# The opening of a transformer layer kernel: squares summed in fours, later copies, a dot row and sums interleaved, and the context's columns loaded later

## The chip, the cores and the metric

The kernel runs on one core of a Trainium2 chip. A core has a matrix engine (TensorE, PE in the profile, its weight loads PEld), VectorE (DVE), ScalarE (ACT), GpSimd (POOL) and SyncE (SP), which here issues the loads. The engines run side by side, each through its own queue in order. The metric is the device time of one execution in microseconds (us).

## The reference

One layer of a backbone over 512 latent tokens and 256 context tokens, width 1024. All vectors are modulated: two conditioning vectors, `c` for latent tokens and `c_ctx` for context tokens, go through SiLU and a matrix `w_ada` of 1024 x 9216, which gives shifts, scales and gates. The opening of the kernel belongs to the first sublayer:

```python
mx = jnp.split((jax.nn.silu(c) @ w_ada + b_ada)[:, None, :], N_MOD, axis=-1)
mc = jnp.split((jax.nn.silu(c_ctx) @ w_ada + b_ada)[None, None, :], N_MOD, axis=-1)
...
def rms_norm(x, w):
    y = xf * lax.rsqrt(jnp.mean(xf * xf, axis=-1, keepdims=True) + EPS)
    return (y * w.astype(jnp.float32)).astype(x.dtype)
...
h = modulate(rms_norm(h_in, norm_w), shift, scale)      # h * (1 + scale) + shift
return h_in + 0.5 * gate * swiglu(h, w1, w3, w2)
```

After it come token mixing (latent attention in one head group, a gated chunk MLP in the other) and a second such sublayer; the output is the latent stream.

## The kernel before

All activations lie transposed, features on the 128 partitions and tokens along the row: `x` holds eight blocks k of 128 features with 768 columns, in two groups g of 256 latent and 128 context tokens each. A product in fp32 precision is made of three matmuls over high and low parts (`hh`, `hl` for the activation, `oph`, `opl` for the weight; `op5h` and `op5l` are the pair of k=5). The opening, up to about 67 us, has to get from nothing to the first four output blocks of the first up-projection, and works on the eight feature blocks as they come.

**Loads.** SP issues in the written order: x's latent columns in five loads; then for each block k a unit of three: scale (a block of `w_ada` for TensorE, three buffers), shift (a block of `w_ada` for VectorE, two k to a tile), raw (the weights of the first products, three buffers). `first_units(k)` issues the three. The context's columns of x come in two loads of four blocks: the first behind the units of k = 0, 1, 2, the second inside the unit of k = 3, between its scale and its shift.

**Spread vectors.** TensorE spreads both SiLU vectors over all partitions (L499, into `big`), and `put_cb(w)` on ScalarE copies them to `cb`, where the dot products with the shifts read them. The same two banks later hold the first products.

**Norm.** `square0(0, k)` makes the square of block k of the latent columns: on ScalarE, except that of k = 3, which VectorE makes, and that of k = 7, of which each engine makes a half. Squares lie in a pool of four buffers (`sqx0`), which the context's squares and the pair of k=5 use too. VectorE adds squares, and `sums` (L460) lets TensorE add over the partitions by a matmul with ones, each into the two halves of the columns (`sumx`). Before: squares 0 and 1 are added and summed, 2 and 3 are added and summed, 4, 5 and 6 are added, 7 stands alone; `late_sums(g)` sums these last two for half g. `root(g)` on ScalarE and `steps(g)` on VectorE make the reciprocal root.

**Modulation of block d.** `ada_row(d)` (L320, sixteen records on TensorE) multiplies both vectors with the scale block; `ada_copy(d)` takes the row out of PSUM on ScalarE; `ada_col` (L329) turns it into a column, and ScalarE makes of it the factor `a`. `ada_sum(d, which)` on VectorE is the dot product of the shift block with a spread vector (tile `junk`, 128x1024), and `ada_s` on ScalarE adds the bias. `which` is 0 for latent and 1 for context tokens.

**Block k's operand.** `first_x` (VectorE, `hfull`) multiplies x, the root and the factor; `first_h` (ScalarE) adds the shift and rounds to `hh`; `first_l` (VectorE) makes `hl`. `first_half(g)` (L580) are the products of k = 0 by halves; `step_mm(k)` (L588) those of the others; `first_ctx(k)` (L573) those of the context's columns.

**Steps.** `step_open(k)` stands at the head of each step on TensorE: the column of block k+1 and the dot row of block k+2; `step_mm(k)` ends it. Between them the code writes what VectorE and ScalarE do for the next blocks. The context's squares are made in this time, by `square1(j)` on ScalarE (four blocks j over the 256 columns), added by `ctx_add(a, b)` on VectorE into the third, folded once, and summed by TensorE in step 4, ahead of `step_mm(4)`.

The order on ScalarE, VectorE and TensorE is the written one throughout the opening, as is SP's. A buffer of a pool is given by a planner, which runs through the program with modelled times, and an instruction that needs a buffer waits until its last reader is done. Behind the opening most of the kernel is ordered by hand as well; between the two feed-forward sublayers some parts of the token mixing (lines 1443 to 1612) are ordered by the planner.

Of the kernel before, what the change touches and what calls it, by code (L numbers as in the profile page):

```python
# [9 lines left out]
F32 = mybir.dt.float32  # L10
# [23 lines left out]
W1 = 2 * NFIRST * P  # L34
# [139 lines left out]
def layer_kernel(ctx: ExitStack, tc: tile.TileContext, xT, wfirst, wst, wada, wuq, wkpe, cols, wrope, vnw, rope, out):  # L174
    nc = Core(tc)
# [18 lines left out]
    def big():  # L194
        return half[0].tile([P, 2, 512], F32, tag="big", bufs=2, name=f"big_{nc.next_id()}")
# [59 lines left out]
    load_x = lambda k, n, c: pin(nc.sync.dma_start(four(x[:, k : k + n, :], c), four(xT[:, k : k + n, :], c)))  # L255
    for k, n in ((0, 2), (2, 2), (4, 2), (6, 1), (7, 1)):
        load_x(k, n, slice(0, 256))
    sblk, units = [], []

    def first_units(k, between=None):  # L260
        ra = sp.tile([P, D], F32, tag="sa", bufs=3, name=f"scale_{k}")
        pin(nc.sync.dma_start(ra, wada[k][:, :D]))
        if between:
            between()
        if k % 2 == 0:
            pool, tag, bufs = (sp, "sb", 1) if k == 4 else (st.raw_pool, "block", BLOCKS)
            sblk.append(pool.tile([P, 2048], F32, tag=tag, bufs=bufs, name=f"shift_{k}"))
        rs_ = sblk[-1][:, (k % 2) * D : (k % 2) * D + D]
        pin(nc.sync.dma_start(rs_, wada[k][:, D:]))
        rw = st.raw()  # L270
        pin(nc.sync.dma_start(rw[:, :W1], wfirst[k]))
        units.append((ra, rs_, rw[:, :W1]))

    for k in range(3):
        first_units(k)
    load_x(0, 4, slice(256, 384))
    warm = mm()
    nc.scalar.activation(epsc2, epsc, AF.Silu)
    for i in range(4):
# [38 lines left out]
    def ada_row(d):  # L318
        for kt in range(NK):
            pin(nc.tensor.matmul(pa[0:2, :P], sc[:, kt, :], units[d][0][:, kt * P : kt * P + P], start=kt == 0, stop=kt == NK - 1))  # L320

    def ada_copy(d):
        row = sp.tile([2, P], F32, tag="row", name=f"row_{d}")
        nc.scalar.copy(row, pa[0:2, :P])
        return row

    def ada_col(row, d):
        o = pcol[:, 2 * d : 2 * d + 2]
        pin(nc.tensor.matmul(o, row, ident[0:2, 0:2], start=True, stop=True))  # L329
        nc.scalar.activation(  # L330
            pairs[0][1][:, d, :], o, AF.Identity, bias=b1n[:, d : d + 1], scale=col[:, COL_N1 + d : COL_N1 + d + 1])

    def ada_sum(d, which):
        ada_dot(units[d][1], d, which, accs[:, d, which : which + 1])

    def ada_s(d, which):
        nc.scalar.activation(mod_s[0][which][:, d : d + 1], accs[:, d, which : which + 1], AF.Identity, bias=col[:, d : d + 1])

    def ada_shift(d, which):
        ada_sum(d, which)  # L340
        ada_s(d, which)
# [110 lines left out]

    def square1(j):
        sq = sp.tile([P, 512], F32, tag="sqx0", bufs=4, name=f"sq0_1{j}")
        nc.scalar.activation(
            sq.rearrange("p (q c) -> p q c", c=P), x.rearrange("p k (g c) -> p (k g) c", g=2)[:, 4 * j : 4 * j + 4, 256:384], AF.Square)
        return sq

    def sums(dst, sq, first, last):
        pin(nc.tensor.matmul(dst[:, :256], ones, sq, start=first, stop=last))  # L460
# [40 lines left out]
    sumx = [mm(), mm()]  # L501
    half_of = lambda g: slice(256 * g, 256 * g + 256)
    put_cb = lambda w: nc.scalar.copy(cb[:, w, :], bb[w].rearrange("p g c -> p (g c)"))
    for k in (0, 2):
        sa = square0(0, k)
        sb = square0(0, k + 1)
        nc.vector.tensor_add(sa, sa, sb)
        for g in range(2):
            sums(sumx[g], sa[:, half_of(g)], k == 0, False)
    put_cb(0)  # L510
    sq = [square0(0, k) for k in (4, 5, 6)]
    nc.vector.tensor_add(sq[0], sq[0], sq[1])
    nc.vector.tensor_add(sq[0], sq[0], sq[2])
    nc.vector.tensor_scalar_add(b1, col[:, COL_B : COL_B + 72], 1.0)
    sq[1] = square0(0, 7)
    put_cb(1)
    nc.vector.tensor_mul(b1n, b1[:, NK : 2 * NK], col[:, COL_N1 : COL_N1 + NK])
    ops = {}

    def oph(k):  # L520
        ops[k] = st.pair() if k != OPS else [sp.tile([P, 512], F32R, tag="sqx0", bufs=4, name=f"op5{p}") for p in "hl"]
        nc.scalar.copy(ops[k][0], units[k][2])

    def opl(k):
        nc.vector.tensor_sub(ops[k][1], units[k][2], ops[k][0].bitcast(F32))

    r0, v = rstd_tiles(0)
    rs = [v]
# [1 line left out]
    def late_sums(g):  # L530
        for i in range(2):
            sums(sumx[g], sq[i][:, half_of(g)], False, i == 1)

    def root(g):
        rstd_root(sumx[g], r0[:, half_of(g)])

    def steps(g):
        rstd_steps(sumx[g], r0[:, half_of(g)], v[:, half_of(g)])

    late_sums(0)  # L540
    root(0)
    ada_row(0)
    row = ada_copy(0)
    ada_col(row, 0)
    late_sums(1)
    oph(0)
    steps(0)
    ada_shift(0, 0)
    root(1)
    first_x(0, 0, 0)  # L550
    first_h(0, 0, 0)
    opl(0)
    first_units(3, lambda: load_x(4, 4, slice(256, 384)))
    ada_row(1)
    row = ada_copy(1)
    first_l(0, 0, 0)
# [2 lines left out]
    first_x(0, 0, 1)  # L559
    opl(1)  # L560
    first_h(0, 0, 1)
    pbs = bigs(4)
    pcs = []

# [37 lines left out]
    sqs = []  # L602
# [10 lines left out]
    ada_sum(2, 0)  # L613
    first_l(1, 0)
    oph(2)
    opl(2)
    ada_s(2, 0)
    for k in (4, 5):
        first_units(k)

    step_open(1)
    first_x(2, 0)
    first_h(2, 0)
    row = ada_copy(3)
    ada_sum(0, 1)
    for j in (0, 1):
        sqs.append(square1(j))
    first_l(2, 0)
    ada_sum(3, 0)
    oph(3)  # L630
    opl(3)
    ada_s(3, 0)
    ada_s(0, 1)
    sqs.append(square1(2))
    step_mm(1)

    step_open(2)
    first_x(3, 0)
    first_h(3, 0)
    sqs.append(square1(3))  # L640
    row = ada_copy(4)
    ctx_add(2, 0)
    first_l(3, 0)
    ada_sum(4, 0)
    oph(4)
    opl(4)
    ada_s(4, 0)
    ada_sum(1, 1)
    ada_s(1, 1)
    step_mm(2)  # L650
    for k in (6, 7):
        first_units(k)

    step_open(3)
    first_x(4, 0)
    first_h(4, 0)
    row = ada_copy(5)
    ctx_add(3, 1)
    first_l(4, 0)
    ada_sum(5, 0)  # L660
    oph(5)
    opl(5)
    ada_s(5, 0)
# [8 lines left out]
    first_h(5, 0)  # L672
    row = ada_copy(6)
    first_l(5, 0)
    ada_sum(6, 0)
    rc = rstd_tiles(1)
    rstd_root(sumc, rc[0])
    rstd_steps(sumc, *rc)
    rs.append(rc[1])
    nc.scalar.activation(epsc2, epsc, AF.Silu)  # L680
    ada_s(6, 0)
    for j in (0, 1):
        first_x(j, 1)
# [530 lines left out]
    sums = [SsqAcc(npool, 384, nc.vector) for _ in range(2)]  # L1214
# [220 lines left out]
    def between():  # L1435
        if next(slots) and tiny and next(tiny[0], tiny) is tiny:
            tiny.pop(0)
# [223 lines left out]
    steps = [(h, t) for h in range(HEADS) for t in range(4)]  # L1661
# [156 lines left out]
    for i in range(3, LAST):  # L1818
        j = i - 3
# [31 lines left out]
    i = LAST  # L1851
# [360 lines left out]
```

## Time and profile before

| | |
|---|---|
| median of 3 runs | 1134.43 us (1132.75 to 1135.95) |
| the profiled execution | 1134.94 us, its span 1133.2 us |
| granted TensorE clock | 1.000 |
| TensorE busy | 1124.0 us (99%) |
| VectorE, ScalarE, GpSimd busy | 906.4, 540.5, 306.8 us |
| moved by DMA | 125.89 MB, 111 GB/s in the mean |

The profile is of one execution. Ends of matmuls in it are modelled, so TensorE's work is best read from the starts. A row of the timeline has the start and the duration in us, the engine, the line of the code (L59 stands for everything that is recorded in written order), the operation, what is written and read, the count of merged instructions, and in brackets how long the engine was idle before and what it waited for.

### The profile page before, as it was taken

What the parts mean: (1) busy time and instruction counts of PE and PEld (TensorE: products, weight loads), DVE (VectorE), ACT (ScalarE), POOL (GpSimd) and SP (SyncE); (2) the same over time, 40 slices, a digit from 0 to 9 for tenths busy, and PEclk for the clock granted to TensorE, in tenths of its full rate; (3) what the DMA queues carried; (4) which work ended last, traced back from release to release, by engine and by line L of the source; (5) the groups of instructions that cost most, each with busy time, mean ns of one, the idle gap of its engine ahead of it and who ended that gap; (6) DMA issues with size and microseconds to landing.
All of it is one profiled execution on the core that took longest, in us unless ns stands there. A gap on an engine that the chain in (4) does not pass through costs nothing.

```text
span 1133.2 us, 18761 instructions
## 1 busy us (share of the span) xinstructions
PE 1124.0 (99%) x7078; PEld 1072.6 (95%) x7078; DVE 906.4 (80%) x1666; ACT 540.5 (48%) x1120; POOL 306.8 (27%) x268
## 2 busy tenths in 40 slices
PE   9999999999999999999999999999999999999998
PEld 7799999999999999999988889999999989898997
DVE  6989999888888779867746889978886868686884
ACT  6555422431344214445745559975544535353451
POOL 0002402321333023300018327740013435152330
PEclk9999999999999999999999999999999999999999
DMA  9630353244333755322243111002131422233312
GB/s 343 212 116 19 118 181 132 102 143 146 116 127 138 246 192 187 112 69 66 84 149 109 40 38 39 20 27 86 56 107 46 147 75 91 98 111 112 113 38 93
DMA packets 35674, 125.89 MB, mean 111 GB/s; under 512 B 3712, under 2 KB 10624, under 8 KB 30976
## 3 DMA queue, kind: packets, MB, share of 16 engines
q1 hardware_dynamic: 35440, 124.63, 32.2%
q8 instruction: 56, 0.92, 0.3%
q14 instruction: 34, 0.28, 0.1%
q10 hardware_dynamic: 144, 0.06, 0.0%
HBM read 122.58 MB, written 2.10 MB: 110 GB/s over the span
## 4 chain that ended last, share of the span: by engine, by line
PE 89%; DVE 6%; POOL 2%; issue 1%; ACT 1%; DVEq 0%; ACTq 0%; POOLq 0%
PE mm L59 54%; PE one L59 19%; PE big L59 7%; PE big L588 2%; PE mm L320 1%; DVE opl L59 1%; PE mm L573 1%; PE mm L170 1%; PE mm L169 1%; PE mm L168 1%; DVE hfB L59 1%; DVE m8k L59 1%; PE big L499 0%; POOL ut L1501 0%; PE mm L280 0%
## 5 line engine op out<-in xcount | busy, mean ns | idle before, releaser
L59 DVE TENSOR_TENSOR opl<-block,oph 128x512 fp32r<-128x512 f32 x216 | 192.3, 898 | 35.4 <-ACT oph L59 31.8
L59 POOL TENSOR_TENSOR block<-block 128x512 f32<-128x512 f32 x69 | 105.2, 1525 | 391.8 <-DVE opl L59 389.1
L59 ACT CAST oph<-block 128x512 fp32r<-128x512 f32 x216 | 133.8, 622 | 117.3 <-PE mm L59 85.4
L59 PE MATMUL mm<-gh,oph 128*128 128x384 f32 (+1 forms) x440 | 155.2, 353 | 0.0
L59 PE MATMUL mm<-gl,oph 128*128 128x384 f32 (+1 forms) x440 | 154.9, 352 | 0.0
L59 PE MATMUL mm<-gh,opl 128*128 128x384 f32 (+1 forms) x440 | 154.9, 352 | 0.0
L59 DVE SCALAR_TENSOR_TENSOR x<-mm,g,x 128x256 f32<-128x256 f32 (+2 forms) x185 | 85.4, 499 | 49.0 <-PE mm L59 48.9
L59 ACT CAST oph<-raw 128x512 fp32r<-128x512 f32 x115 | 69.9, 620 | 78.1 <-PE mm L59 56.3
L59 PEld LDWEIGHTS mm<-gh,opl 128*128 128x128 f32 x440 | 82.6, 188 | 5.7
L59 PEld LDWEIGHTS mm<-gh,oph 128*128 128x128 f32 x440 | 82.6, 188 | 5.6
L59 PEld LDWEIGHTS mm<-gl,oph 128*128 128x128 f32 x440 | 82.6, 188 | 5.5
L59 POOL TENSOR_TENSOR block<-s,block 128x512 f32<-128x512 f32 x35 | 47.8, 1367 | 142.3 <-DVE opl L59 141.4
L59 DVE TENSOR_TENSOR opl<-raw,oph 128x512 fp32r<-128x512 f32 x115 | 77.7, 691 | 8.8 <-ACT oph L59 8.0
L59 PE MATMUL mm<-hh,oph 128*128 128x384 f32 x192 | 64.5, 336 | 0.0
L59 PE MATMUL mm<-hl,oph 128*128 128x384 f32 x192 | 64.2, 334 | 0.0
L59 PE MATMUL mm<-hh,opl 128*128 128x384 f32 x192 | 64.1, 334 | 0.0
L59 DVE SCALAR_TENSOR_TENSOR junk<-raw,cb 128x1024 bf16<-128x1024 f32 x48 | 62.1, 1308 | 0.0
L59 POOL TENSOR_TENSOR s<-block 128x512 f32<-128x512 f32 x34 | 50.2, 1477 | 21.0 <-DMA block<-wst 21.0
L59 PE MATMUL one<-hh,oph 128*128 128x384 f32 x144 | 48.1, 334 | 0.0
L59 PE MATMUL one<-hl,oph 128*128 128x384 f32 x144 | 48.1, 334 | 0.0
L59 PE MATMUL one<-hh,opl 128*128 128x384 f32 x144 | 48.1, 334 | 0.0
L59 DVE SCALAR_TENSOR_TENSOR raw<-raw,cb 128x1024 f32<-128x1024 f32 x32 | 41.0, 1288 | 7.7 <-DMA raw<-wada 7.4
(683 smaller groups left out, 3430.5 us busy)
## 6 DMA issues: line engine op xcount, KB each, us to landing
raw<-wst SPq DMA_DIRECT2D x77, 512.0 KB, 3.7
block<-wst SPq DMA_DIRECT2D x36, 1024.0 KB, 4.9
raw<-wada SPq DMA_DIRECT2D x56, 512.0 KB, 4.1
scale<-wada SPq DMA_DIRECT2D x8, 512.0 KB, 8.7
shift<-wada SPq DMA_DIRECT2D x8, 512.0 KB, 9.2
x<-xT SPq DMA_DIRECT2D x5, 512.0 KB, 6.1
raw<-wfirst SPq DMA_DIRECT2D x8, 256.0 KB, 8.3
out<-x SPq DMA_DIRECT2D x7, 256.0 KB, 2.2
```

What stands on the lines that cost most here:

```text
L59: return lambda *a, **k: self.tc.keep_in_program_order(f(*a, **k))
L168: nc.tensor.matmul(out, lh, rh, start=first, stop=False, skip_group_check=more)
L169: nc.tensor.matmul(out, lh, rl, start=False, stop=False, skip_group_check=more)
L170: nc.tensor.matmul(out, ll, rh, start=False, stop=last, skip_group_check=more)
L320: pin(nc.tensor.matmul(pa[0:2, :P], sc[:, kt, :], units[d][0][:, kt * P : kt * P + P], start=kt == 0, stop=kt == NK - 1))
L573: pin(nc.tensor.matmul(o, l[:, c], r, start=k == 0 and m == 0 and w == 0, stop=k == NK - 1 and m == 2, skip_group_check=True))
L588: pin(nc.tensor.matmul(two(pbs[i]), l[:, c], lat(r, k), start=False, stop=k == NK - 1 and m == 2, skip_group_check=True))
```

## The change

The opening's order is written anew; nothing is computed by other means.

- Squares 0 to 3 are made first and added up (three adds on VectorE), and one sum per half stands for the two of before. Then squares 4 to 7 are made, all ahead of the adds of 4, 5 and 6.
- `put_cb(0)` moves behind the squares, `put_cb(1)` behind the first root.
- The rounded weights of k = 0 (`oph(0)`), the first dot product with the shift and the root's steps come ahead of the first dot row; the sums of the second half come between that row and its column.
- The units of loads are split into functions. The unit of k = 4 comes earlier, the context's columns go behind unit 4 and behind scale 5; the shifts of k = 6 and 7 go last.
- The context's squares move from steps 1 and 2 to the end of step 2 and to step 3, the adds of them into step 3, the second vector's dot product of block 1 to an earlier place in step 2, and in step 4 the dot product of block 6 behind the context's root.

```diff
+    def first_scale(k):
         ra = sp.tile([P, D], F32, tag="sa", bufs=3, name=f"scale_{k}")
         pin(nc.sync.dma_start(ra, wada[k][:, :D]))
-        if between:
-            between()
+        units.append([ra])
+
+    def first_shift(k):
...
+    def first_units(k):
+        first_scale(k)
+        first_shift(k)
+        first_raw(k)
     for k in range(3):
         first_units(k)
-    load_x(0, 4, slice(256, 384))
...
-    for k in (0, 2):
-        sa = square0(0, k)
-        sb = square0(0, k + 1)
-        nc.vector.tensor_add(sa, sa, sb)
-        for g in range(2):
-            sums(sumx[g], sa[:, half_of(g)], k == 0, False)
-    put_cb(0)
-    sq = [square0(0, k) for k in (4, 5, 6)]
+    sq = [square0(0, k) for k in range(4)]
+    for i, j in ((1, 0), (3, 2), (3, 1)):
+        nc.vector.tensor_add(sq[i], sq[i], sq[j])
+    for g in range(2):
+        sums(sumx[g], sq[3][:, half_of(g)], True, False)
+    sq = [square0(0, k) for k in (4, 5, 6, 7)]
     nc.vector.tensor_add(sq[0], sq[0], sq[1])
     nc.vector.tensor_add(sq[0], sq[0], sq[2])
+    sq[1] = sq[3]
+    put_cb(0)
     nc.vector.tensor_scalar_add(b1, col[:, COL_B : COL_B + 72], 1.0)
-    sq[1] = square0(0, 7)
-    put_cb(1)
...
     late_sums(0)
     root(0)
+    put_cb(1)
+    oph(0)
+    ada_sum(0, 0)
+    steps(0)
     ada_row(0)
     row = ada_copy(0)
+    ada_s(0, 0)
+    late_sums(1)
     ada_col(row, 0)
-    late_sums(1)
-    oph(0)
-    steps(0)
-    ada_shift(0, 0)
     root(1)
     first_x(0, 0, 0)
     first_h(0, 0, 0)
     opl(0)
-    first_units(3, lambda: load_x(4, 4, slice(256, 384)))
+    first_units(3)
...
     first_h(0, 0, 1)
+    first_units(4)
+    load_x(0, 4, slice(256, 384))
...
     ada_s(2, 0)
-    for k in (4, 5):
-        first_units(k)
+    first_scale(5)
+    load_x(4, 4, slice(256, 384))
+    first_shift(5)
+    first_raw(5)
     step_open(1)
...
     ada_sum(0, 1)
-    for j in (0, 1):
-        sqs.append(square1(j))
...
     ada_s(0, 1)
-    sqs.append(square1(2))
     step_mm(1)
     step_open(2)
     first_x(3, 0)
     first_h(3, 0)
-    sqs.append(square1(3))
     row = ada_copy(4)
-    ctx_add(2, 0)
+    ada_sum(1, 1)
     first_l(3, 0)
     ada_sum(4, 0)
     oph(4)
     opl(4)
     ada_s(4, 0)
-    ada_sum(1, 1)
     ada_s(1, 1)
+    for j in (0, 1):
+        sqs.append(square1(j))
     step_mm(2)
     for k in (6, 7):
-        first_units(k)
+        first_scale(k)
+        first_raw(k)
+    for k in (6, 7):
+        first_shift(k)
     step_open(3)
     first_x(4, 0)
     first_h(4, 0)
     row = ada_copy(5)
-    ctx_add(3, 1)
+    for j in (2, 3):
+        sqs.append(square1(j))
+    ctx_add(2, 0)
     first_l(4, 0)
     ada_sum(5, 0)
+    ctx_add(3, 1)
     oph(5)
     opl(5)
     ada_s(5, 0)
...
     first_l(5, 0)
-    ada_sum(6, 0)
     rc = rstd_tiles(1)
     rstd_root(sumc, rc[0])
     rstd_steps(sumc, *rc)
     rs.append(rc[1])
     nc.scalar.activation(epsc2, epsc, AF.Silu)
+    ada_sum(6, 0)
     ada_s(6, 0)
```

More of the change, by code (lines that the diff above doesn't have):

```diff
@@ L257, in layer_kernel @@
         load_x(k, n, slice(0, 256))
-    sblk, units = [], []
-    def first_units(k, between=None):
+    sblk, units, raws_ = [], [], []
+    def first_scale(k):
         ra = sp.tile([P, D], F32, tag="sa", bufs=3, name=f"scale_{k}")
         pin(nc.sync.dma_start(ra, wada[k][:, :D]))
-        if between:
-            between()
+        units.append([ra])
+    def first_shift(k):
         if k % 2 == 0:
@@ L269, in first_units, with first_raw @@
         pin(nc.sync.dma_start(rs_, wada[k][:, D:]))
+        units[k].append(rs_)
+    def first_raw(k):
         rw = st.raw()
         pin(nc.sync.dma_start(rw[:, :W1], wfirst[k]))
-        units.append((ra, rs_, rw[:, :W1]))
+        raws_.append(rw[:, :W1])
+    def first_units(k):
+        first_scale(k)
+        first_shift(k)
+        first_raw(k)
     for k in range(3):
         first_units(k)
-    load_x(0, 4, slice(256, 384))
     warm = mm()
@@ L521, in oph @@
         ops[k] = st.pair() if k != OPS else [sp.tile([P, 512], F32R, tag="sqx0", bufs=4, name=f"op5{p}") for p in "hl"]
-        nc.scalar.copy(ops[k][0], units[k][2])
+        nc.scalar.copy(ops[k][0], raws_[k])
     def opl(k):
-        nc.vector.tensor_sub(ops[k][1], units[k][2], ops[k][0].bitcast(F32))
+        nc.vector.tensor_sub(ops[k][1], raws_[k], ops[k][0].bitcast(F32))
     r0, v = rstd_tiles(0)
```

## Prediction, made before the changed kernel ran

> **What bounds the kernel now.** I read the page first, then the busy time by stretches, then the opening's timeline engine by engine.
>
> ```profile
> PE 1124.0 (99%) x7078; PEld 1072.6 (95%) x7078; DVE 906.4 (80%) x1666; ACT 540.5 (48%) x1120; POOL 306.8 (27%) x268
> ...
> PE 89%; DVE 6%; POOL 2%; issue 1%; ACT 1%; DVEq 0%; ACTq 0%; POOLq 0%
> ```
>
> The first line is the busy time of each engine, the second the chain that ended last. TensorE is the bound nearly everywhere, so an edit of the opening counts only by what it does to TensorE: matmuls taken out, waits taken out, waits put in. Next, one stretch of the busy times (length, then busy PE, PEld, DVE, ACT, POOL).
>
> ```profile
> 49.00:67.00 18.00, 18.00 (x124) 16.62 (x124) 17.38 (x33) 8.95 (x22) 0.00 (x0) 1.00 0.54 177
> ```
>
> TensorE has no gap in these last 18 us of the opening, but VectorE is busy 17.38 of them: it keeps pace and can't give back a delay there. What can be won lies before, in the timeline of the opening (start, duration, engine, line, operation, count, idle before and its releaser).
>
> ```profile
> 1.03 3.78 PE L280 MATMUL mm<-ones 128*128 128x256 f32 x8 [1.03 <-DVE nhalf L224]
> ...
> 6.26 0.69 DVE L59 TENSOR_TENSOR sq<-sq,sq 128x512 f32<-128x512 f32 x1 [5.26 <-ACT sq L59]
> ...
> 6.39 0.63 ACT L59 ACTIVATE sq<-x 128x512 f32<-128x512 f32 x1 [0.17 <-DMA x<-xT]
> 6.87 0.68 DVE L59 TENSOR_TENSOR sq<-x 128x512 f32<-128x512 f32 x1
> ...
> 7.67 1.01 ACT L59 COPY cb<-big 128x1024 f32<-128x1024 f32 x1 [0.65 <-PE big L499]
> ...
> 9.26 1.89 PE L460 MATMUL mm<-sq,ones 128*128 128x256 f32 x8
> ...
> 10.32 0.94 ACT L59 ACTIVATE sq<-x 128x512 f32<-128x512 f32 x2 [0.59 <-PE mm L460]
> ...
> 11.70 0.42 DVE L59 TENSOR_TENSOR sq<-x 128x256 f32<-128x256 f32 x1
> ...
> 11.73 1.14 PE L460 MATMUL mm<-sq,ones 128*128 128x256 f32 x4 [0.58 <-DVE sq L59]
> ...
> 12.80 1.91 PE L320 MATMUL mm<-scale,sc 128*2 128x128 f32 x16
> ...
> 15.05 0.38 PE L329 MATMUL mm<-ident,row 2*128 2x2 f32 x2 [0.34 <-ACT row L59]
> ...
> 15.47 0.35 ACT L59 ACTIVATE a<-mm,b1n,col 128x2 f32<-128x2 f32 x1 [0.47 <-PE mm L329]
> ...
> 16.42 1.91 PE L320 MATMUL mm<-scale,sc 128*2 128x128 f32 x16
> ...
> 16.90 0.50 ACT L59 ACTIVATE hh<-hfull,s 128x256 fp32r<-128x256 f32 x1
> ...
> 17.43 0.49 DVE L59 SCALAR_TENSOR_TENSOR hl<-hfull,s,hh 128x256 fp32r<-128x256 f32 x1 [0.38 <-ACT hh L59]
> ...
> 18.26 0.74 PE L580 MATMUL big<-hh,oph 128*128 128x256 f32 x4
> ```
>
> Between 9.26 and 18.26 TensorE waits 0.58 us for a sum of squares and 0.34 us for the copied row; the eight records at 9.26 are the sums of two pairs. All that the opening holds is therefore 0.58 + 0.34 + half of 1.89 (0.95), some 1.9 us.
>
> **The first sums.** Four squares are added first, so four records stand for eight: 0.95 us of TensorE work goes. VectorE's square of k=3 needs the load that ScalarE's third square waits for (6.39), so it runs from 6.39 to 7.07 (0.68); the adds of 0.69 us follow some 0.6 us apart (6.26 to 6.87 is that step), and the third reads the second's result: start 8.4, end 9.1. TensorE is at the spread vectors until 9.26, so it waits for nothing here.
>
> **The second sums.** The pool of squares has four buffers. At 10.32 ScalarE's square waits for TensorE's first four records of sums, which release a buffer. In the new order the same four records read the buffer of square 3, the last of the four that comes free, and the eighth square takes it: again at 10.32. VectorE does half of that square (0.42), and both adds of the second group now stand behind it in its queue: 10.33, then about 10.7 and 11.4 (the second add reads the first's result), end 12.1. TensorE starts the late sums at about 12.15, 0.4 us later than 11.73. If the planner gives the eighth square the buffer of square 1 instead (free at 9.1, when square 6 asks too), it is 11.73 as before; so 0 to +0.45, and I take +0.4, since buffers come free in this order and square 6 asks first. The freed 0.95 us thus turns into a longer wait: TensorE idles from about 10.3 to 12.15.
>
> **Row and sums interleaved.** From 11.73 to 16.42 TensorE needed 4.69 us, with the 0.34 us and some 0.06 us around the row copy idle. Second sums now fill that hole: 12.15 + 4.69 - 0.4 = 16.4, no gain against 16.42. The scale's column moves behind those sums, from 15.05 to 16.0, so `a` starts at 16.4 instead of 15.47; then x's product (0.49, as the row at 17.43), hh (0.50) until 17.85, hl (0.49) until 18.4. TensorE wants hh at 18.2 and hl one group (0.58) later: 0.4 us of cover in both, and what goes beyond it costs one to one. Copies of the spread vectors behind the squares: the first (1.01) starts behind the eighth square's half, near 10.7, and ends near 11.7, before its reader, the dot product with the shift, which VectorE reaches after 12.1; the second runs while VectorE makes the first root's steps. Cost nothing, for the same cover. Opening in sum: 0, from -0.4 to +0.5.
>
> **SP's queue.** Of each unit three transfers; context's x (two of 512 KB) goes behind unit 4's and behind scale 5.
>
> ```profile
> 14.74 0.61 SPq L262 DMA_DIRECT2D scale<-wada  x1
> ...
> 23.95 1.91 PE L320 MATMUL mm<-scale,sc 128*2 128x128 f32 x16
> ...
> scale<-wada SPq DMA_DIRECT2D x8, 512.0 KB, 8.7
> ...
> x<-xT SPq DMA_DIRECT2D x5, 512.0 KB, 6.1
> ```
>
> Scale 3 goes out at 14.74 and with the median 8.7 us lands near 23.4, used at 23.95: cover about 0.5. With one x transfer fewer ahead of it this can only widen. The x transfers wait on SP behind scales that need a freed buffer, the last of them that of the third dot row, which is over before the fourth starts at 23.95; so they leave by about 24 and land by about 30 (6.1), and the squares of them move to 34 and later. No queue comes late: 0. The shifts of 6 and 7 no longer hold raw 6 and scale 7 back: 0 too, since TensorE has no wait there.
>
> **Context's squares and their adds.** Here a cost lies on the path. Step 3 before:
>
> ```profile
> 26.45 1.15 ACT L59 ACTIVATE sq<-x 128x512 f32<-128x512 f32 x2
> ...
> 32.11 1.22 DVE L59 SCALAR_TENSOR_TENSOR junk<-shift,cb 128x1024 bf16<-128x1024 f32 x1
> ...
> 33.85 0.38 PE L329 MATMUL mm<-ident,row 2*128 2x2 f32 x2
> ...
> 35.32 0.34 ACT L59 ACTIVATE a<-mm,b1n,col 128x2 f32<-128x2 f32 x1
> ...
> 36.48 0.72 ACT L59 ACTIVATE hh<-hfull,s 128x512 fp32r<-128x512 f32 x1 [0.82 <-DVE hfull L59]
> ...
> 37.10 0.24 ACT L59 COPY row<-mm 2x128 f32<-2x128 f32 x1
> ...
> 37.23 0.75 DVE L59 SCALAR_TENSOR_TENSOR hl<-hfull,s,hh 128x512 fp32r<-128x512 f32 x1 [0.19 <-ACT hh L59]
> ...
> 37.90 1.22 DVE L59 SCALAR_TENSOR_TENSOR junk<-shift,cb 128x1024 bf16<-128x1024 f32 x1
> ...
> 39.05 0.69 DVE L59 TENSOR_TENSOR op5l<-raw,op5h 128x512 fp32r<-128x512 f32 x1
> 39.65 0.68 DVE L59 TENSOR_TENSOR sq<-sq,sq 128x512 f32<-128x512 f32 x1
> 40.37 0.42 DVE L59 TENSOR_TENSOR sq<-sq 128x256 f32<-128x256 f32 x1
> 40.71 0.74 DVE L59 SCALAR_TENSOR_TENSOR hfull<-x,a,v 128x512 f32<-128x512 f32 x1
> ...
> 41.11 0.70 PE L460 MATMUL mm<-sq,ones 128*128 128x256 f32 x2
> ```
>
> The folded square ends at 40.37 + 0.42 = 40.8, and TensorE reads it at 41.11 ahead of step 4's matmuls: 0.3 us of cover. After: step 2's last dot product ends near 33.5 (32.11 + 1.22, and 0.2 for the other one pulled ahead of it), ScalarE then makes two bias columns and squares 0 and 1 (1.15) until about 35.2, `a` until 35.45, x's product (0.74, as at 40.71) 35.5 to 36.25, hh 36.3 to 37.0, the row, and only then squares 2 and 3 (1.15): 37.1 to 38.25. VectorE's first add (2 with 0) waits for square 2 until 37.75, with nothing to do since 36.25, and the queue stands behind it: add 37.75, hl 38.35, dot product 39.0, add 40.15, low operand 40.75, add 41.35, fold 42.05 to 42.5 (steps by starts: 0.6 for an add or operand, 0.67 for hl, 1.15 for a dot product). TensorE's sums go from 41.11 to 42.5: **+1.4 us**. Bounds: +1.0 if ScalarE passes the squares 0.4 us sooner, +1.8 if the operand copy for k=5, which needs a square's buffer, adds what it can.
>
> **After that.** VectorE is 42.45 - 40.71, so 1.7 us late, and stays late through a stretch without gaps; where hl of context's k=2 goes to TensorE, there was a wait before:
>
> ```profile
> 53.11 0.19 PEld L573 LDWEIGHTS mm<-hl,oph 128*128 128x128 f32 x1 [0.15 <-DVE hl L59]
> ```
>
> VectorE recovers part (its root steps now go ahead of a dot product, one stall on ScalarE's root less), so I put +0.1 there, between 0 and +0.3. The kernel behind 67 us moves as a block. Sum: 0 + 1.4 + 0.1 = +1.5 us. The profiled execution took 1134.94 us, so 1136.4; the median of the runs shown, 1134.43, is 0.5 below it: **1135.9**. By the bounds: +0.6 to +2.6, so 1135.0 to 1137.0. A measurement tells 0.3% (3.4 us) from no change, so this is no change.
>
> **A gap and the clock.** Two rows bear on whether 1.9 us of idle TensorE slow it down:
>
> ```profile
> 663.19 0.47 PE L59 MATMUL mm<-mixh,oph 128*128 128x512 f32 x1 [1.60 <-ACT uo0h L59]
> 663.50 0.39 PE L59 MATMUL mm<-mixl,oph 128*128 128x512 f32 x1
> 640.00:680.00 40.00, 37.85 (x200) 31.96 (x199) 35.19 (x71) 22.30 (x45) 9.19 (x12) 1.00 0.12 40
> ```
>
> After 1.60 us of idleness the next matmul follows 0.31 us later and the granted clock of the stretch is 1.00. The Trainium skill, page "TensorE: Matmul & The Clock Gate", section "Part 1: The HAM clock gate", has the array fall to half clock after at least one idle window of about 3.4 us; by that rule a gap of 1.9 us costs nothing, and the sum stays; the trace agrees as far as 1.60 us.
>
> **Rivals.**
> *The clock drops in the new gap* (slower). Eight records of 128x256 took 3.78 us at the start and 1.89 us from 9.26, so cold is half pace. It stayed cold for those 3.78 us at least; as long a cold stretch from 12.15 loses half of that, 1.9 us, and up to half of 8.2, 4.1 us, if it lasts as long as from 1.03 to 9.26. With +1.5: 1137.8 to 1140.0, say 1138.5. It decides from a gap longer than the 1.60 us seen to be free, and the new one is. Chance 0.12.
> *The adds come in time* (the change's plain reading): square 2 earlier, or the second sums not behind the eighth square. Then the waits of 0.58 and 0.34 us and the 0.95 us are won in part: 1132.5 to 1134.8. For it speaks that VectorE's and ScalarE's waits in steps 2 and 3 are short; against it the written order, which those engines follow. Chance 0.16.
> *The planner answers.* The order of lines 1443 to 1612 (token mixing, ahead of the stretch from 640 us) isn't written by hand but planned from modelled times, so a changed opening can turn it. TensorE idles 2.15 us in that stretch: winning it with the 1.9 us of the opening gives 1130.4, losing as much again on top of +1.5 gives 1138.1. Nothing in the profile says which. Chance 0.32: 0.11 faster, 0.09 within 0.3%, 0.12 slower.
>
> **How the numbers follow.** The forecast keeps 0.40. Within 0.3%: 0.40 + 0.16 + 0.09 = 0.65; slower: 0.12 + 0.12 = 0.24; faster 0.11. The range runs from 1132.0 (most of the early case) to 1139.0 (most of the clock and planner cases).
>
> **What would show it.** Right: four sum records from 9.26; TensorE's next at 12.1 with a wait on VectorE; the second dot row at 16.4; a wait of over 1 us on VectorE before the two sums of step 4; from there all matmuls about 1.5 us later. Wrong: the late sums at 11.7 or earlier; no wait at step 4; 128x128 dot rows that take near 3.8 instead of 1.91 us (clock); or equal openings and another time in the token mixing (planner).

## The result, and the profile after

The changed kernel takes 1138.27 us (median of 7 executions, 1136.92 to 1141.34) against 1134.35 us before (7 executions, 1132.55 to 1135.95): the ratio is 1.0041, with a 95% interval of 1.0032 to 1.0051. It is slower by about 3.9 us, which a measurement can tell from no change; the forecast was 1135.9 us and "no change". The profiled execution of the changed kernel is its longest, 1141.34 us with a span of 1139.6.

From the page of the changed kernel, the busy time of the engines and the chain that ended last; then, from the busy times by stretches, the one that answers to 49 to 67 us (length, busy PE, PEld, DVE, ACT, POOL, granted clock, DMA share, GB/s):

```profile
PE 1126.7 (99%) x7074; PEld 1073.3 (94%) x7074; DVE 907.6 (80%) x1667; ACT 540.7 (47%) x1120; POOL 306.9 (27%) x268
...
PE 85%; DVE 7%; ACT 2%; issue 1%; DMA 1%; POOL 0%; ACTq 0%; DVEq 0%; POOLq 0%
...
53.00:71.00 18.00, 17.99 (x121) 16.42 (x120) 17.41 (x34) 8.99 (x22) 0.00 (x0) 1.00 0.51 172
```

TensorE is busy for 2.7 us more than before although the change takes matmuls out: a first sign that the same matmuls ran more slowly. The stretch behind the opening looks as it did. The opening itself is told by TensorE's timeline (start, duration, engine, line, operation, count, idle before and its releaser). All lines of the opening lie eight to ten further down than before: L468 are the sums, L328 the dot rows, L337 the column, L590 the first products.

```profile
9.31 1.13 PE L468 MATMUL mm<-sq,ones 128*128 128x256 f32 x4 [0.71 <-DVE sq L59]
12.36 2.08 PE L468 MATMUL mm<-sq,ones 128*128 128x256 f32 x4 [1.92 <-DVE sq L59]
14.37 3.57 PE L328 MATMUL mm<-scale,sc 128*2 128x128 f32 x16
17.87 1.44 PE L468 MATMUL mm<-sq,ones 128*128 128x256 f32 x4
19.24 0.38 PE L337 MATMUL mm<-ident,row 2*128 2x2 f32 x2
19.55 1.91 PE L328 MATMUL mm<-scale,sc 128*2 128x128 f32 x16
```

The four records of the first sums start where they should, and the late sums at 12.36 (forecast 12.15) behind a gap of 1.92 us. Then come rows that are too long, although TensorE waits for nothing inside them: 2.08 instead of 1.14 us for four sums, 3.57 instead of 1.91 us for the first dot row. The second dot row starts 3.13 us later than before (16.42). At 19.55 us the same form takes 1.91 us again. This is a lower clock, not a wait, and the stretches show it. Their edges are laid on the edges of the half-clock stretches, which are 3.41 us or twice that long:

```profile
8.30:11.71 3.41, 1.43 (x7) 0.79 (x5) 2.05 (x5) 2.83 (x5) 0.00 (x0) 1.00 1.05 400
11.71:15.12 3.41, 2.76 (x8) 1.64 (x9) 2.16 (x6) 0.73 (x3) 0.00 (x0) 0.50 1.04 406
15.12:18.53 3.41, 3.41 (x16) 1.97 (x14) 1.13 (x3) 1.70 (x4) 0.00 (x0) 0.50 0.95 372
18.53:21.94 3.41, 3.41 (x26) 2.47 (x25) 1.88 (x4) 1.67 (x5) 0.00 (x0) 1.00 0.80 272
667.07:670.48 3.41, 1.71 (x7) 1.33 (x8) 3.41 (x8) 1.94 (x4) 0.05 (x1) 1.00 0.30 98
670.48:673.89 3.41, 3.41 (x10) 2.74 (x10) 1.14 (x3) 0.00 (x0) 0.00 (x0) 0.50 0.17 60
```

The granted clock is 0.50 from 11.71 to 18.53 us, and once more from 670.48 to 673.89, behind the gap of 1.60 us of which the prediction had said that it costs nothing. The stretch ahead of each fall is one in which TensorE was busy for half of the time or less: 1.43 and 1.71 of 3.41 us. Before, the same gap of 1.60 us lay across an edge:

```profile
658.80:662.21 3.41, 2.42 (x15) 1.73 (x14) 3.38 (x8) 1.59 (x5) 1.23 (x2) 1.00 0.02 5
662.21:665.62 3.41, 2.43 (x11) 2.02 (x12) 3.02 (x6) 0.99 (x3) 0.00 (x0) 1.00 0.42 156
```

These are stretches of the kernel before, with the edges counted on by 3.413 us from the start of its full clock at 6.86 us. Each half of the gap leaves 2.4 us of work in its stretch, and the clock stays full.

The rest of the loss is in step 3. From the timelines of VectorE, ScalarE and TensorE:

```profile
38.57 0.75 DVE L59 SCALAR_TENSOR_TENSOR hfull<-x,a,v 128x512 f32<-128x512 f32 x1 [1.23 <-ACT a L59]
...
40.13 1.15 ACT L59 ACTIVATE sq<-x 128x512 f32<-128x512 f32 x2
...
40.79 0.69 DVE L59 TENSOR_TENSOR sq<-sq,sq 128x512 f32<-128x512 f32 x1 [1.47 <-ACT sq L59]
...
45.31 0.43 DVE L59 TENSOR_TENSOR sq<-sq 128x256 f32<-128x256 f32 x1
...
45.88 0.67 PE L468 MATMUL mm<-sq,ones 128*128 128x256 f32 x2 [1.58 <-DVE sq L59]
```

VectorE stands 1.47 us behind ScalarE's square 2, its fold ends at 45.7, and TensorE waits 1.58 us for it ahead of the two sums of step 4, where it waited for nothing before.

Followed along TensorE in this execution, the delay against before is 3.1 us at the second dot row, 4.8 us at the sums of step 4, 5.9 us at 637 us and 7.5 us at 674 us; between 878 and 906 us some 1.0 us comes back, where the kernel before has short waits of its own that the later arrival absorbs; 6.4 us are left. This is the longest execution; the medians lie 3.9 us apart. The 1.1 us at 637 us are a wait of 1.52 instead of 0.44 us, whose chain goes back to two loads of weights (3.79 and 4.50 us from issue to landing). Behind 80 us the order of the instructions on TensorE, VectorE, ScalarE and GpSimd is that of before.

### The profile page after: what moved, and what is told of

Read it like the earlier page. It is cut to its first block, busy times and chain, and to the rows that moved or that the text cites. A ratio compares the mean times of both kernels' runs of the same rounds, so it can differ in the third digit from the quotient of the medians.

```text
span 1139.6 us, 18757 instructions
## 1 busy us (share of the span) xinstructions
PE 1126.7 (99%) x7074; PEld 1073.3 (94%) x7074; DVE 907.6 (80%) x1667; ACT 540.7 (47%) x1120; POOL 306.9 (27%) x268
## 4 chain that ended last, share of the span: by engine, by line
PE 85%; DVE 7%; ACT 2%; issue 1%; DMA 1%; POOL 0%; ACTq 0%; DVEq 0%; POOLq 0%
PE mm L59 54%; PE one L59 19%; PE big L59 7%; PE mm L583 1%; DVE opl L59 1%; PE big L598 1%; PE mm L170 1%; PE mm L168 1%; PE mm L169 1%; DMA raw<-wst 1%; DVE hfB L59 1%; DVE m8k L59 1%; DVE opl L140 0%; DVE ut L1522 0%; DVE hfA L59 0%
```

## The experiments

Two theories at first. **C**: the gap of 1.92 us makes TensorE's clock fall, and this is the larger part of the loss. **S**: the late fold of context's squares makes the rest. Rivals were **V**, that VectorE's and ScalarE's chain in the opening is late by itself; **X**, that the context part makes the loss and the opening is made up for later; and **Q**, that the new order of the loads costs something. All medians below are of 6 or 11 executions, and each group of kernels ran beside the kernel before on the same chip (1134.04, 1133.44 and 1134.29 us in the three groups). Each execution also lists its mean granted clock; half clock for one stretch of 3.41 us shows as 0.998.

### Work in the gap

```diff
     for g in range(2):
         sums(sumx[g], sq[3][:, half_of(g)], True, False)
+    for _ in range(4):          # 2 in the second kernel
+        pin(nc.tensor.matmul(two(pa[:, :256]), ones, ones2, start=True, stop=True))
```

Four matmuls of ones, expected:

> The changed kernel with four matmuls of ones (128x256, results never read) behind the first sums, 4 x 0.47 = 1.9 us, so that TensorE has work from 10.4 to 12.3 us. Theory C (the idle 1.92 us of TensorE made its granted clock fall to half for 6.83 us): the clock stays full through the opening, the late sums start within 0.2 us of 12.36, the first dot row takes 1.91 instead of 3.57 us and the second starts near 16.5 instead of 19.55; the wait of 1.6 us ahead of the sums of step 4 stays; 1135.2 to 1136.2 us. Rival V (VectorE's and ScalarE's chain in the opening is late by itself, and the clock only goes along with it): the second dot row stays at 19 or later and the time at 1138.

Two of them, expected:

> As the kernel with four matmuls of ones, but with two (0.95 us), so that about 1.0 us of idleness is left ahead of the late sums. Theory C with a threshold (it takes more than about 1.3 us idle of a stretch of 3.4 us): the clock stays full, second dot row near 16.5, 1135.2 to 1136.2 us. If any gap of about 1 us behind the first sums is enough: half clock again for 3.4 or 6.8 us, second dot row 18 to 19.5, 1137 to 1138.3 us. Rival V: 1138.

Measured: 1136.36 us with four (ratio to before 1.0017, interval 1.0009 to 1.0026) and 1135.63 us with two (1.0014, 1.0005 to 1.0023). TensorE's timeline with four, then the late sums and the second dot row with two:

```profile
10.23 1.89 PE L518 MATMUL mm<-ones 128*128 128x256 f32 x8
12.31 1.13 PE L468 MATMUL mm<-sq,ones 128*128 128x256 f32 x4 [0.19 <-DVE sq L59]
13.38 1.91 PE L328 MATMUL mm<-scale,sc 128*2 128x128 f32 x16
...
16.58 1.91 PE L328 MATMUL mm<-scale,sc 128*2 128x128 f32 x16
...
42.93 0.67 PE L468 MATMUL mm<-sq,ones 128*128 128x256 f32 x2 [1.58 <-DVE sq L59]
```

```profile
12.20 1.13 PE L468 MATMUL mm<-sq,ones 128*128 128x256 f32 x4 [1.05 <-DVE sq L59]
...
16.46 1.91 PE L328 MATMUL mm<-scale,sc 128*2 128x128 f32 x16
```

The late sums start when they did, VectorE is no faster, and yet the second dot row comes 3.0 us earlier. V falls: with the same chain on VectorE and ScalarE the opening costs 0.2 us at most (second dot row at 16.58 and 16.46, against 16.42 before). Half of the gap (1.05 us) does no harm, so it is not the gap as such. The time is the expected one in the second kernel and 0.2 us above the band in the first. Each against its own runs of before, the filled gap wins 1.6 and 2.3 us of the 3.9. The wait of 1.58 us in step 4 stays, as expected. So does the kernel's own gap of 1.60 us: both profiles fall to half clock once, behind it, at 665.70 and 665.57 us.

### Each half of the change alone

The opening of the change in the kernel before (squares, sums, copies, dot row; loads and context as before), and the context part alone (loads, squares, adds, with the opening of before):

> The kernel before with the opening of the change alone (four squares added ahead of their sums, copies of the spread vectors behind the squares, row and sums interleaved); loads, squares and adds of context stay as before. Theory C: gap of 1.9 us, half clock for 3.4 to 6.8 us, second dot row at 18.5 to 19.6, no wait over 0.5 us ahead of the sums of step 4 unless VectorE is late; all behind 20 us later by about 3; 1137.0 to 1137.8 us. Rival X (the context part makes the loss, the opening is made up for later): within 0.7 us of the kernel before, 1133.7 to 1135.1 us.

> The kernel before with the context part of the change alone: context's x loaded later, its squares and adds in steps 2 and 3 at the places of the change; the opening as before. Theory S (the fold of context's squares comes too late): clock full throughout, a wait of 1.0 to 1.8 us on VectorE ahead of the two sums of step 4, all behind it later by that; 1135.4 to 1136.2 us. Rival C alone (only the clock counts, the wait of step 4 is made up behind it): within 0.5 us of the kernel before. Rival Q (the order of the loads holds something up behind 60 us): over 1136.5 us, with a DMA as releaser.

Measured: 1136.12 us for the opening alone (1.0019, 1.0011 to 1.0028) and 1135.94 us for the context part alone (1.0015, 1.0005 to 1.0024). The opening alone, TensorE's timeline and two stretches:

```profile
12.29 1.22 PE L460 MATMUL mm<-sq,ones 128*128 128x256 f32 x4 [1.92 <-DVE sq L59]
13.45 3.44 PE L320 MATMUL mm<-scale,sc 128*2 128x128 f32 x16
...
18.18 1.91 PE L320 MATMUL mm<-scale,sc 128*2 128x128 f32 x16
```

```profile
9.78:13.19 3.41, 1.50 (x7) 0.87 (x5) 2.64 (x6) 1.39 (x3) 0.00 (x0) 1.00 1.03 404
13.19:16.60 3.41, 3.41 (x17) 1.86 (x16) 1.79 (x5) 1.90 (x3) 0.00 (x0) 0.50 1.03 404
...
661.73:665.14 3.41, 1.76 (x12) 1.18 (x11) 3.41 (x8) 1.62 (x4) 1.23 (x2) 1.00 0.01 2
```

The same gap of 1.92 us, but one stretch at half clock instead of two, and the second dot row at 18.18: the cost of the same gap differs from execution to execution. The gap at 664 us lay with 1.76 us of work in its stretch and did not lower the clock. The median is 0.9 us below the expected 1137.0, because not every execution falls, or falls twice: 2 of 11 had a mean clock of 1.000 (mean 1134.49 us), 5 had 0.998 (1135.70), 3 had 0.997 (1137.41) and one 0.995 (1138.81). The time follows the clock. X falls: the opening alone loses 2.1 us of the 3.9, about half, which is less than the larger part that C gave to the clock.

The context part alone, TensorE's only new wait:

```profile
42.33 0.67 PE L468 MATMUL mm<-sq,ones 128*128 128x256 f32 x2 [1.22 <-DVE sq L59]
```

1.22 us, within S's 1.0 to 1.8, and the time within its band. The clock was not full throughout, as S had expected: the profile falls at 665.49 us, behind the kernel's own gap, and 9 of 11 executions had 0.998, against 13 of 33 of the kernel before beside them. At equal clock the difference is 1.0 us (two executions at 1.000: 1134.47 against 1133.47) and 1.4 us (at 0.998: 1136.03 against 1134.62), about the wait; the rest of the 1.9 us is the more frequent fall, which may be chance. Q falls: no wait on a load is added in the opening. The two halves add up: 2.1 and 1.9 us, against 3.9 for the whole change. That they do so to 0.1 us is partly luck.

### A gap alone, and the other gap filled

Is it the gap, or something else in the new opening? Two operations of VectorE without effect make a gap in the kernel before; three matmuls of ones fill the gap at 661 us.

```diff
     nc.vector.tensor_add(sq[0], sq[0], sq[2])
+    for _ in range(2):
+        nc.vector.tensor_tensor(sq[0], sq[0], sq[0], ALU.max)
```

> The kernel before, with nothing of the change, but two operations of VectorE of 0.69 us that change nothing (the maximum of a sum of squares with itself) ahead of the late sums, so that TensorE waits from 11.15 to about 13.1 us instead of to 11.73. Theory C (a gap of about 1.9 us halves the granted clock): half clock for 3.4 to 6.8 us somewhere in 11 to 20 us, second dot row at 19.5 to 21.2 us, the mean clock of nearly every run 0.998 or lower, 1137.1 to 1138.8 us median. Rival V (only the chain of VectorE counts): clock full in the opening, second dot row at 17.8, 1135.4 us.

```diff
     uo_half(0)()
+    for _ in range(3):
+        pin(nc.tensor.matmul(two(ob[1][:, :256]), ones, ones2, start=True, stop=True))
     og(3, og3, 0, P0)
```

> The kernel before, with three matmuls of ones (1.4 us, results never read) in the gap of 1.60 us at 661.6 us. The runs of the kernel before fall in two groups: 19 with a mean clock of 1.000 (mean 1133.47 us) and 13 with 0.998 (1134.62). Theory C2 (where the gap of 1.60 us lies within one window of the clock's, it costs half clock for 3.4 us there): all runs at 1.000, none at 0.998, median 1133.3 to 1133.6. Rival N (the clock's fall has nothing to do with that gap): the same two groups, median 1134.0.

The gap alone: 1135.59 us (1.0011, 1.0003 to 1.0020), less than C had asked for and close to V's number. Six of 11 executions had 0.998, but so had 11 of 28 of the kernel before, so this run alone does not tell which gap lowered the clock. Its profiled execution had the longer gap of 2.29 us and a full clock:

```profile
12.30 1.10 PE L460 MATMUL mm<-sq,ones 128*128 128x256 f32 x4 [2.29 <-DVE b L59]
13.33 1.91 PE L320 MATMUL mm<-scale,sc 128*2 128x128 f32 x16
```

```profile
7.89:11.30 3.41, 2.12 (x12) 1.56 (x10) 2.58 (x4) 3.21 (x6) 0.00 (x0) 1.00 1.05 393
11.30:14.71 3.41, 2.41 (x17) 1.74 (x18) 2.07 (x7) 0.47 (x1) 0.00 (x0) 1.00 1.03 404
```

So C was wrong in the form "a gap of 1.9 us lowers the clock". What counts is the busy share of a fixed stretch, and here an edge cut the gap in two. The edges lie elsewhere in each execution.

The other gap filled: 1132.82 us, 0.6 below the kernel before on the same chip (ratio 0.9993, 0.9984 to 1.0002). Ten of 11 executions had a mean clock of 1.000 and one 0.999 (the profiled one, whose only half clock lies in its last 1.2 us); of 88 executions of the kernel before in the three groups, 40 had 0.998, and they were 1.2 us longer than those at 1.000 (1133.47 and 1134.62 us in the first group). The kernel before thus pays for its own gap in nearly every second execution. N, that the fall has nothing to do with that gap, does not hold. Of the gap 0.30 us is left in the profile:

```profile
661.62 1.46 PE L59 MATMUL big<-ones 128*128 128x256 f32 x6
663.38 0.47 PE L59 MATMUL mm<-mixh,oph 128*128 128x512 f32 x1 [0.30 <-ACT uo0h L59]
```

The next two kernels put the filled gap at 661 us into the kernel with the gap alone and into that with the opening alone, so that only the opening can lower the clock.

> The kernel before with the two extra operations of VectorE ahead of the late sums (gap of about 2 us in the opening), and with the three matmuls of ones in the gap of 661 us, so that only the opening's gap can lower the clock. Theory C (a gap of 1.9 to 2.3 us in the opening lowers it where it lies within one window): more than half of the runs at a mean clock of 0.998 or 0.999, those 1.2 us or more slower than the runs at 1.000, median 1133.9 to 1135.5 us. Rival M (in the kernel with the gap alone all falls of the clock came from the gap at 661 us): all runs at 1.000, 1133.2 to 1133.8 us.

> The kernel before with the opening of the change alone, and with the three matmuls of ones in the gap of 661 us. Theory C: the falls of the clock that come from the opening's gap of 1.92 us stay: more than half of the runs below 1.000, with 0.998 and 0.997 for one and two windows, median 1134.3 to 1135.8 us; the profile with half clock in 11 to 20 us where the gap lies within one window. Rival M: all at 1.000 and 1132.9 to 1133.6 us.

The gap alone: 1134.52 us, 5 of 11 executions below 1.000, three of them at 0.998 (mean 1136.29 us, against 1134.14 at 1.000) and two at 0.999. The opening alone: 1135.56 us, 9 of 11 at 0.998 (1136.05). M does not hold for the opening alone, whose profile below has half clock right behind the opening's gap. With the gap alone no execution at 0.998 was profiled: that the opening's gap lowered the clock there is inferred, since the trace shows no other gap of that size, and it fell in fewer than the half of the executions that C expected. One stretch of the first profile, without a fall behind it, then two of the second:

```profile
8.45:11.86 3.41, 1.83 (x9) 1.27 (x8) 2.37 (x4) 2.56 (x5) 0.00 (x0) 1.00 1.05 403
```

```profile
8.68:12.09 3.41, 1.29 (x6) 0.68 (x4) 2.08 (x4) 2.67 (x5) 0.00 (x0) 1.00 1.03 401
12.09:15.50 3.41, 3.03 (x10) 1.77 (x11) 2.17 (x6) 0.92 (x2) 0.00 (x0) 0.50 1.03 404
```

The opening of the change has a second, shorter gap (0.58 us in the second profile, 0.71 in the changed kernel) ahead of the first sums, which adds to the idle time of the stretch:

```profile
9.42 1.13 PE L460 MATMUL mm<-sq,ones 128*128 128x256 f32 x4 [0.58 <-DVE sq L59]
12.47 2.08 PE L460 MATMUL mm<-sq,ones 128*128 128x256 f32 x4 [1.92 <-DVE sq L59]
```

### Useful work in the gap

The first dot row needs only its scale, which has landed by 10.8 us. In the opening of the change alone, half of it goes ahead of the late sums:

```diff
+    ada_row(0, range(4))
     late_sums(0)
...
-    ada_row(0)
+    ada_row(0, range(4, NK))
```

> The opening of the change alone (context as before), with the first four of the eight matmuls of the first dot row moved into the gap behind the first sums, where their operand has landed (10.8 us). Theory C: no gap over 0.7 us in the opening, clock full, late sums at 12.2 to 12.4, second dot row near 16.0 (before: 16.42; opening of the change alone: 18.5 with half clock); 1133.4 to 1134.2 us median, 2 us less than the opening alone with its 1136.1. Rival V: 1135.5 to 1136.1 us.

Measured: 1133.91 us (1.0004, 0.9996 to 1.0013), 2.2 us less than the opening alone (1.6 us less, each against its own runs of before). TensorE:

```profile
10.72 1.04 PE L320 MATMUL mm<-scale,sc 128*2 128x128 f32 x8 [0.50 <-DMA scale<-wada]
12.14 1.13 PE L460 MATMUL mm<-sq,ones 128*128 128x256 f32 x4 [0.38 <-DVE sq L59]
...
15.70 1.91 PE L320 MATMUL mm<-scale,sc 128*2 128x128 f32 x16
...
24.00 1.25 PE L320 MATMUL mm<-scale,sc 128*2 128x128 f32 x10 [0.69 <-DMA scale<-wada]
```

The second dot row is 0.7 us earlier than before, and the gain is gone at 24.00, where the fourth dot row waits 0.69 us for its load. The clock is full in the opening; the profile falls once, at 663.65 us behind the kernel's own gap, and 5 of 11 executions had 0.998. With the loads in the order of before, the reordered opening had nothing to win.

### The fold of context's squares

Two ways to take away the wait in step 4, both on the changed kernel with four matmuls of ones in the gap. First, context's sums, their root and what hangs on it go behind the first half of step 4's matmuls:

> The changed kernel with the four matmuls of ones behind the first sums, and the sums of context's squares, their root and what hangs on it moved behind the first half of step 4's matmuls (some 4 us later). Theory S (the wait of 1.6 us ahead of the sums of step 4 is what is left of the loss once the clock is full): no such wait, and no other over 0.5 us before 67 us; 1.5 us less than with the matmuls of ones alone: 1134.0 to 1134.9 us median, 1133.3 to 1133.8 in runs with a mean clock of 1.000. Rival D (VectorE is too late anyway, the wait turns up at context's low parts, 50 to 60 us): 1135.4 us or more.

Measured: 1137.45 us, 1.1 us more than with the matmuls of ones alone (1.7 us more, each against its own runs of before). The wait at step 4 is gone; three others stand in its place, the low and high parts of context's blocks:

```profile
50.71 0.39 PE L585 MATMUL mm<-hl,oph 128*128 128x256 f32 x1 [0.52 <-DVE hl L59]
54.57 0.38 PE L585 MATMUL mm<-hh,oph 128*128 128x256 f32 x1 [0.55 <-ACT hh L59]
55.91 0.39 PE L585 MATMUL mm<-hl,oph 128*128 128x256 f32 x1 [0.95 <-DVE hl L59]
```

This came as rival D had it, but it does not decide between S and D: the edit itself makes the root, and all that VectorE does with it, some 4 us later. A second kernel therefore takes only the stall off VectorE, and leaves the sums where they are:

```diff
-    ctx_add(2, 0)
     first_l(4, 0)
+    ctx_add(2, 0)
```

> The changed kernel with the four matmuls of ones behind the first sums, and in step 3 VectorE's first add of context's squares behind the low part of k=4 instead of ahead of it, so that VectorE no longer stands 1.47 us behind square 2. Theory S (that stall makes the fold late and with it TensorE's sums): the wait ahead of the two sums of step 4 falls from 1.58 us to 0.3 to 0.7, nothing appears in its place before 67 us, 0.9 to 1.3 us less than with the matmuls of ones alone (1136.4): 1135.0 to 1135.4 us. Rival D (VectorE's lateness turns up at context's low parts): less than 0.4 us won, a new wait between 50 and 60 us.

```profile
36.97 0.75 DVE L59 SCALAR_TENSOR_TENSOR hl<-hfull,s,hh 128x512 fp32r<-128x512 f32 x1 [0.79 <-ACT hh L59]
37.64 0.69 DVE L59 TENSOR_TENSOR sq<-sq,sq 128x512 f32<-128x512 f32 x1
```

```profile
42.07 0.67 PE L468 MATMUL mm<-sq,ones 128*128 128x256 f32 x2 [0.92 <-DVE sq L59]
```

The stall of 1.47 us becomes one of 0.79 us, the wait of 1.58 us becomes 0.92, and the time falls from 1136.36 to 1135.50 us (executions at full clock: 1135.03 to 1134.21), with nothing new behind it. 0.7 us less stall, 0.7 us less wait, 0.8 to 0.9 us less time: the rows show S, and the times agree with it, though the intervals of the two kernels overlap (ratios to before 1.0009 to 1.0026 and 1.0001 to 1.0019). The edit won less of the wait than expected, and the time is 0.1 us above the band.

### A wait that could not be moved

The gap at 661 us was taken to end with VectorE's eviction of the bank P0. Writing the tile ahead of it to another bank should have freed P0 earlier:

```diff
-    og(2, og2, 1, P0)
+    og(2, og2, 1, ob[1])
...
-    evac_lat(P0, 5, 1)
+    evac_lat(ob[1], 5, 1)
```

> The kernel before, with the sixth output tile of the output projection (second half of unit 2) in the other half of the two-bank tile that holds the fifth, instead of in the bank P0, so that the seventh (the first of unit 3) doesn't wait for VectorE's eviction of the sixth. If that eviction ends the 1.60 us wait at 661 us: the matmuls start when the low operand is there, gap 0.2 to 0.6 us, no fall of the clock behind it (all runs at 1.000), of which up to 1 us comes back as a wait for the keys' low part ahead of the first scores: 1131.5 to 1132.9 us. If the wait is for ScalarE's copy (uo0h), as the releaser in the trace has it: gap of 1.4 us or more as before, 1133.4 us, two groups of runs.

Measured: 1137.07 us (1.0029, 1.0017 to 1.0040), slower.

```profile
661.50 0.46 PE L59 MATMUL big<-mixh,oph 128*128 128x512 f32 x1 [4.13 <-DVE x L59]
```

The two halves of that tile are one tile to the waits: TensorE stands idle for 4.13 us, and the matmul into the second half starts 0.1 us behind the end of the eviction of the first. All 6 executions were below a clock of 1.000. Whether the gap of 1.60 us ends with the eviction of P0 or with ScalarE's copy `uo0h`, which most traces name, stays open.

## Why the prediction was wrong

**Opening, the sums.** Right but for one wait. Four records from 9.3 us; the late sums at 12.36 (12.15), since the eighth square takes the buffer that TensorE frees at 10.4 and both adds stand behind it. The gap was forecast at 1.9 us and measured 1.92. The sum had no wait ahead of the first sums, because TensorE would be at the spread vectors until 9.26. In the changed kernel's profile they took 3.89 instead of 4.81 us, since the first full clock came at 4.88 instead of 6.86 us, and 0.71 us of waiting stood there. The start of the sums did not move, but the stretch got more idle time. Where the first full clock came at 6.37 us or later, the new opening had no such wait.

**Row and sums interleaved.** Right with a full clock: second dot row at 16.58 and 16.46 with the gap filled, against a forecast of 16.4. The low and high parts behind it keep their cover.

**A gap and the clock.** This is the step that failed. "... by that rule a gap of 1.9 us costs nothing, and the sum stays; the trace agrees as far as 1.60 us": the one gap of 1.60 us in the trace of before happened to lie across the edge of two stretches, and it was taken for a proof about gaps of that length. In other executions of the same kernel the same gap costs 1.2 us. In the changed kernel the new gap put TensorE at half clock for 6.83 us in the profile, and the second dot row 3.1 us back, where the sum had 0. In the medians the term is 1.6 to 2.3 us (the gap filled) or 2.1 us (the opening alone), most of the 2.4 us by which the forecast was short. The rule of the Trainium skill (page "TensorE: Matmul & The Clock Gate", section "Part 1: The HAM clock gate") speaks of an idle window of about 3.4 us that runs freely. Stretches of 3.41 us are in these traces, and so is their free running: the first full clock starts between 4.47 and 7.09 us. But no window had to be idle throughout: one that was idle for half was enough.

**SP's queue.** Right: 0 in the opening. The wait of 1.52 us at 637 us in the profiled execution, whose chain goes back to loads, was also there in one other of the 14 traces (1.46 us, opening alone with the filled gap) and at most 0.50 us in the rest; whether the change makes it more frequent stays open.

**Context's squares.** Right: forecast +1.4 (1.0 to 1.8), measured 1.22 us with the context part alone and 1.58 us in the changed kernel. The stall behind square 2 was forecast at 1.5 us and measured 1.47. **After that**: forecast +0.1 us; the wait for `hl` of context's k=2, 0.15 us before, is 0.22 us in the changed kernel.

**The rivals.** *The clock drops in the new gap* was given 0.12 and 1138.5 us; it is what happened, at 1138.27. That its price is so near was partly luck: it took the length of the cold stretch from the start of the kernel (3.78 to 8.2 us), while half clock comes here in stretches of 3.41 us, and not in every execution. What was wrong is its condition: the point from which it decides is no length of a gap, but a stretch half idle. *The adds come in time* did not happen. *The planner answers* did not either, since the order behind 80 us is unchanged: it was given 0.32, more than the clock.

**What stays open.** The few executions of the opening alone with a mean clock of 1.000 (two of each kernel) are still 1.0 us (alone) and 1.5 us (with the filled gap) above the mean of the kernel before at 1.000 beside them; none of them was profiled. Executions of the kernel before at 1.000 themselves spread over 1132.32 to 1134.73 us beside the opening alone, so two executions say little. The wait near 634 us, which is 0.2 to 0.5 us in twelve traces and 1.5 us in two, could be it.

## What to carry to other kernels

Work taken off TensorE beside a wait turns into idleness, and idleness has a second price: look at the sum of the gaps in every stretch of the clock's length, not at the longest gap, and remember that where the edges fall differs from execution to execution, so one trace without a fall proves nothing. Such a gap is best closed with a piece of work that is ready (here half a dot row), and matmuls nobody reads keep the clock full too; the same cure on a gap that had been there all along gave the shortest median of all the kernels here, 1132.82 us, if by less than can be told from no change. And a step put behind another in an engine's queue takes the stalls of that queue along: one exchanged line took 0.7 us off the wait.

## What the runs showed of the hardware

In 14 traces, with stretches of 3.413 us counted on from the first full clock, and the last 10 us of each execution left out, every full-clock stretch in which TensorE was idle for 1.71 us or more (eleven, up to 2.60 us) was followed by half clock, and none in which it was idle for 1.65 us or less. The ends fit: there half clock followed 1.88 us and more, and not 1.67 us and less. The page of the Trainium skill named above has a window of this length. That half of it decides, these runs add, as far as the modelled ends of matmuls allow. A stretch at half clock was followed by full clock when it held at most 0.37 us of idleness (eleven cases), and by a second one at half clock in the one case with 0.66 us, the changed kernel's. So idle time that goes on in the next stretch can cost a second one: 3.1 us of delay at the second dot row here.
